# Early maxima and constants beside the second unit, one PSUM tile for the sample columns, free buffers for residual and normed rows, gates between key pieces

## The chip, the cores and the metric

The kernel runs on one core of a Trainium2 chip. The metric is the device time of one execution, in microseconds (us). Three runs of the kernel before took 2386.42, 2399.36 and 2394.37 us, median 2394.37. A further execution was taken by the hardware profiler, and all trace rows come from that one.

The engines have short names throughout: PE (TensorE, matrix products) with PEld (its weight loads, beside the products), DVE (VectorE), ACT (ScalarE), POOL (GpSimd), SP (SyncE, which here issues nearly all DMAs). Each works through its own queue in order.

## The reference

One inference step of two residual layers over a prompt of 2048 rows and a sample of 32 rows (8 sequences of 4), 1024 columns wide, in float32:

```python
def run_trunk(x, fox_attend, ...):
    for l in range(DEPTH):                   # DEPTH = 2
        if l % 2 == 0:
            out, ... = even_mixer(rmsnorm(x, norm_even[i]), w_in_even[i], ...)
        else:
            out, ... = odd_mixer(rmsnorm(x, norm_odd[i]), w_in_odd[i], ...)
        x = x + out
    return rmsnorm(x, final_norm), ...

def even_mixer(h, w_in, ...):
    qa, fa, ia, ga, qb, kb, vb, gb, fb = split(h @ w_in)
    f = lb + (1.0 - lb) * sigmoid(fa)
    o_a = head_rmsnorm(gated_linear_chunked(qa, 1 - f, ia, log(f), hgrn_s0)) * silu(ga)
    o_b = fox_attend(qb, kb, vb, log_sigmoid(fb + b_fox)) * silu(gb)
    return concatenate([o_a, o_b]) @ w_out

def odd_mixer(h, w_in, w_gate, b_gate, gla_gain, w_out, gla_s0):
    q, k, v, g, r = split(h @ w_in)
    log_f = log_sigmoid(r @ w_gate + b_gate) / 16
    o = gated_linear_chunked(q * dk ** -0.5, k, v, log_f, gla_s0)
    return (head_rmsnorm(o, gla_gain) * silu(g)) @ w_out
```

The even layer's second half is an attention with forgetting (causal softmax for the prompt, paged cache for the sample). Keys, values, log forget values and states are outputs too.

## The kernel before

**Arithmetic.** TensorE multiplies float16. An activation or weight is scaled by a power of two and written as a sum of two float16 parts, high and low; a product is three matmuls (`mm3`, L583 to L585: high by high, high by low, low by high). Splitting off the parts (one ACT copy, one DVE subtraction) is `split_evac` (L578, L579) for the first norm's rows, L1762 to L1766 for the mixer's output rows (`y_pieces`, loaded at L1752), and L348 to L356 for weights.

**Halves and units.** The prompt goes through the dense work in two halves of 1024 rows; half 0 has the 32 sample rows beside it, as columns 1024 to 1055 of the activation tile `act`. Dense work comes in *units* of some 256 output columns. A unit is a pair: four preparing steps and a run. The steps are: step 0 fetches the weights (L330), step 1 measures their maximum (four DVE reductions L295 over parts, one L297 over their results), step 2 spreads the maximum over the partitions with a matmul against the identity (`spr_...`, L282) and turns it into a power of two, and step 3 splits the weights. The run is a generator of pieces on PE: `proj_fm` (names pf_) gives features by rows, piece by piece of columns (`segs`: three of 352 in half 0, two of 512 in half 1, 24 matmuls each); `proj_tm` (names pt_) gives rows by features, 128 rows a tile in pairs of tiles, with `few_rows` for the 32 sample rows (names pS_; it first copies the sample's columns of `act` into a tile `sam`, L622, and its matmuls are L627).

In the even layer the units are taken in the order Av, Ag, Aqf, Aqf1, Bq, ... (unit 0 to unit 4 of half 0). In phase_odd, units 0 to 3 are the even layer's output projection for half 0 and units 4 to 7 that for half 1 (`out_units`: pt_o0 to pt_o3); then come the odd layer's Cv, Cqk, Cg for each of four heads, from unit 8.

**What sets the order.** The Python code is traced into a program, and a planner then orders each engine's instructions when the kernel is built: it takes them in traced order as their priority, works with planned times, and fills planned idle room with later instructions that are free to run. An instruction that nothing binds can therefore stand far ahead of its place in the code. `tc.issue_after(x)` binds what is traced inside it behind x, but only instructions of x's own engine: `last_x` (the last load of an input row) binds SP, `last_a` binds ACT, `last_v` (the last DVE subtraction of a split or copy to `sam`) binds DVE. `staged` (L1201) runs units j = a to b and deals out, between the pieces of unit j, the preparing steps of the units after it, from lists `todo` of pairs (unit, step); in unit 0 of half 0 (the case with `beside`) the list is written out by hand. `mux` interleaves two generators by shares, `drain` runs one to its end.

**Buffers.** Tiles are taken by tag from pools with a fixed number of buffers for each; a tile waits for the oldest one of its tag to be given back. In phase_odd: "c2" has 4 buffers (residual tiles `xo`, sums of the sample rows, and, under the tag "th", the results of the square sums), "c4" has 6 (first used by the odd units' queries, keys and gates), "v8" 2 (values of the odd units), "yr" 2 (loads of 1024x256 output columns, then the rows `x1r`). PSUM: "pj" 3 (the pieces of all dense units), "gr" 2, "st" 1, "o" 2.

**The places of the change.**

- *First norm* (`norm_groups`, L410): rows are loaded, squared and summed, scaled by their reciprocal root, transposed by PE in 128x128 blocks (L443) into PSUM tiles of the tags "gr" and "o" by turns, and split into the two parts with the norm's gain. The sample group has eight transposes of 32x128, each with its own pair of split_evac operations of 128x32.
- *Start of the even layer* (`phase_even`): unit 0's run goes beside the norm of half 0 (`handover`); during it, `staged` also deals out the measures of unit 1 to 3 and unit 2's spread and split. After it come the constants of the later phases (`more_consts`, L163 to L244: small loads, some 10 DVE operations on them, masks on POOL), bound behind last_x, last_a and last_v, and then units 1 and 2.
- *Normed rows* (`norm_store`, L510): units 4 to 7 are muxed with `prep(0)`, which takes half 0's rows after the first residual, nine tiles with the sample's first: load x1r (SP, L521), square sum (ACT, L527), mean and root (L406 on DVE, a power on POOL), gain (POOL, L529), split (ACT L534, DVE L535), store to a scratch (SP, L536). One step of the generator loads tile x, norms tile x-1 and splits tile x-2. Afterwards the rows come back transposed (`norm_fetch`, DMA transposes L553) as `act` for the odd units. In half 1 the same runs as `prep(1)` beside the odd units.
- *Residuals* (`out_units`, `ev`): for each pair of tiles a load of the residual (SP, L1802), an addition to the product out of PSUM (DVE, L1803, 128x512), and a store (SP, L1805).
- *Gates* (`mk_qk`): a Cqk unit runs the query pieces (evacuated by ACT, L1907), then for every segment a gate (one matmul `z`, L1893, out of "pj", with Abs on ACT, L1895, and a min on DVE, L1896), then Exp, Ln, Exp over the whole row, and then the key pieces (ACT, L1911).

Of the kernel before, what the change touches and what calls it, by code (L numbers as in the profile page):

```python
# [19 lines left out]
P = 128  # L20
D = 1024
KT = D // P
# [87 lines left out]
def drain(g):  # L110
    for _ in g:
        pass
# [11 lines left out]
class Kern:  # L124
# [286 lines left out]
    def norm_groups(self, pool, pps, act, hf, get_tile, gain, tags=("gr", "o")):  # L411
# [6 lines left out]
        def mk(grp):  # L418
# [15 lines left out]
            def turn(at=None, then=None):  # L434
                c0 = grp[0][0]
                if grp[-1][0] == HALF:
                    self.sam = None
                with ExitStack() as st:
                    for k in range(KT):
# [69 lines left out]

    def norm_store(self, pool, hf, tiles, gain):  # L510

# [25 lines left out]

        for x in range(len(todo) + 2):
            if x > 1:
                split(x - 2)  # L540
            if x < len(todo):
                load(x)
            if 0 < x <= len(todo):
                norm(x - 1)
            yield 1000
# [89 lines left out]
    def silu2(self, wp, dst, ps, n, nm, c):  # L635

        nc = self.nc
        th = wp.tile([P, 512], F32, tag="th", name=f"th_{nm}")
        nc.scalar.activation(dst, ps, AF.Copy, scale=c)
        nc.scalar.activation(th[:, :n], dst, AF.Tanh, scale=0.5)  # L640
        nc.vector.scalar_tensor_tensor(dst, th[:, :n], 1.0, dst, ALU.add, ALU.mult)
# [421 lines left out]
    def phase_even(self):  # L1063
# [4 lines left out]
        with pool("act", side="right") as ap, pool("w", side="right") as w0, pool("wl", side="right") as wp1, \  # L1068
# [31 lines left out]
            for hf in range(2):  # L1100
# [11 lines left out]
                if hf == 0:  # L1112
# [21 lines left out]
                    first = self.handover(list(zip(steps, turns)), dense(0, 1), last)  # L1134
                    drain(first)
                    with tc.issue_after(self.last_x.ins), tc.issue_after(self.last_a.ins), \
                            tc.issue_after(self.last_v.ins):
                        self.more_consts(wp)
                else:
                    self.sx_odd = self.gain_scale(self.g_odd, pps, "pj", "o")  # L1140
# [8 lines left out]
                cost = 20800.0  # L1149
                drain(dense(1, 3))  # L1150
                drain(mux(lin(0), LIN_E[hf], dense(3, 5), 2 * cost))
# [49 lines left out]
    def staged(self, us, a, b, beside=None):  # L1201
# [13 lines left out]
        for j in range(a, b):  # L1215
            if j:
                todo = [[(j + 3, 0), (j + 2, 1)], [(j + 2, 2)], [(j + 2, 3)]]
            elif beside is None:
                todo = [[(2, 0), (1, 3)], [(3, 0)], [(2, 3)]]
            else:  # L1220
                todo = [[(1, 0)], [(1, 1)], [(2, 0), (1, 2), (1, 3)], [(3, 0)], [(2, 1), (2, 2), (2, 3)]]
            for n, c in enumerate(us[j][1](self.ready.pop(j))):
# [564 lines left out]
    def out_units(self, hf, layer, act, wpool, wp, pps, x2=None, done=None):  # L1787
# [4 lines left out]
        def mk(u):  # L1792
# [3 lines left out]
            def ev(ps, g, cnt, m):  # L1796
                c0 = self.ttiles(hf)[g][0]
                c = undo[-1 if m < P else 0][:m]
                if x2 is None:
                    t = wp.tile([P, 2, 256], F32, tag="c2", name=f"xo{layer}{hf}{u}{g}")  # L1800
                    src = self.rows(hf, c0, m * cnt, layer == 0)[:, cs].rearrange("(g p) d -> p g d", g=cnt)
# [22 lines left out]
    def odd_half(self, hf, act, wpool, wp, pps, S):  # L1824
# [59 lines left out]
        def mk_qk(h):  # L1884
            def run(W):
                nm = f"C{hf}{h}"

                def gate():
                    f[h], u = c4("f" + nm), c4("u" + nm)
                    ff = f[h]  # L1890
                    for c0, m in self.segs(hf):
                        ps = pps.tile([P, 512], F32, tag="pj", name=f"z{nm}{c0}")
# [12 lines left out]
                if hf == 0:  # L1905
                    nc.vector.tensor_scalar(self.q_undo[h], c, SCALE, None, ALU.mult)
                yield from self.proj_fm(pps, act, W, 0, P, hf, lambda ps, c0, m: nc.scalar.activation(  # L1907
                    q[h][:, c0 : c0 + m], ps, AF.Copy, scale=self.q_undo[h]), nm + "q")
                gate()
                yield Z_C  # L1910
                yield from self.proj_fm(pps, act, W, P, P, hf, lambda ps, c0, m: nc.scalar.activation(  # L1911
                    k[h][:, c0 : c0 + m], ps, AF.Copy, scale=c), nm + "k")

# [26 lines left out]
    def phase_odd(self):  # L1940
# [4 lines left out]
        with pool("act2", side="right") as ap, pool("w2", side="right") as w0, pool("yr2", side="right") as y0, \  # L1945
# [104 lines left out]
            def prep(hf):  # L2050

                def tiles(c0):
                    t = wpool.tile([P, KT, 256], F32, tag="yr", name=f"x1r{hf}{c0}").rearrange("p k t -> p (k t)")
                    return t[:, :D], t[:, D:].bitcast(F16).rearrange("p (x d) -> p x d", x=2)

                return self.norm_store(wp, hf, tiles, grow)

# [103 lines left out]
```

## Time and profile before

| what | value |
|---|---|
| median of 3 runs | 2394.37 us (2386.42 to 2399.36) |
| the profiled execution | 2385.88 us |
| its span in the trace | 2384.2 us |
| mean granted TensorE clock | 0.985 |
| instructions | 58245 |
| HBM read, written | 248.73 MB, 79.63 MB |

How to read the rows that follow. The page gives busy time of each engine and the share of the span. A group reads: line, engine, operation, output<-inputs (names without their numbers), shape, xcount | busy time, mean ns of one | idle time of the engine just before them, and what ended most of it. A timeline row reads: start time in the span, busy time, engine, line, operation, output<-inputs, shape, xcount, and in brackets the idle time of the engine ahead of it with its releaser. SPq rows are DMA issues on SP's queue. A table by stretch gives, for each stretch A:B, its length and then by engine (PE, PEld, DVE, ACT, POOL) the busy time and the number of instructions, followed by the granted PE clock (1.00 is full), the mean busy share of the DMA engines as the view prints it, and GB/s.

### The profile page before, as it was taken

What the parts mean: (1) busy time and instruction counts of PE and PEld (TensorE: products, weight loads), DVE (VectorE), ACT (ScalarE), POOL (GpSimd) and SP (SyncE); (2) the same over time, 40 slices, a digit from 0 to 9 for tenths busy, and PEclk for the clock granted to TensorE, in tenths of its full rate; (3) what the DMA queues carried; (4) which work ended last, traced back from release to release, by engine and by line L of the source; (5) the groups of instructions that cost most, each with busy time, mean ns of one, the idle gap of its engine ahead of it and who ended that gap; (6) DMA issues with size and microseconds to landing.
All of it is one profiled execution on the core that took longest, in us unless ns stands there. A gap on an engine that the chain in (4) does not pass through costs nothing. (4 is left out here: it accounts for less than half of the span.)

```text
span 2384.2 us, 58245 instructions
## 1 busy us (share of the span) xinstructions
PE 2273.3 (95%) x23124; PEld 1617.0 (68%) x23124; DVE 1397.2 (59%) x3231; ACT 1092.9 (46%) x2379; POOL 815.8 (34%) x858
## 2 busy tenths in 40 slices
PE   6999999999999999999999998999899999999998
PEld 5667667864655876655446887777677676666887
DVE  7566566536654638566767444266675655557554
ACT  5334343333333226556667443446545535545333
POOL 1233324112212325234456344043552422322223
PEclk9999999999999999999999999999999999999999
DMA  6221334764441266776874767623233431115453
GB/s 199 63 86 60 93 111 138 193 167 139 144 130 55 78 203 232 241 254 204 267 237 134 248 201 226 158 77 120 83 112 97 114 104 60 43 59 160 154 191 150
DMA packets 358003, 344.89 MB, mean 145 GB/s; under 512 B 90993, under 2 KB 300722, under 8 KB 357730
## 3 DMA queue, kind: packets, MB, share of 16 engines
q1 hardware_dynamic: 356226, 336.64, 46.2%
q8 instruction: 182, 2.98, 0.5%
q0 software_dynamic: 1504, 4.52, 0.5%
q14 instruction: 91, 0.75, 0.1%
HBM read 248.73 MB, written 79.63 MB: 138 GB/s over the span
## 5 line engine op out<-in xcount | busy, mean ns | idle before, releaser
L583 PE MATMUL pt_o<-w_o,act 128*128 128x256 f16 x1024 | 282.9, 276 | 11.6 <-DVE xo L1803 9.2
L585 PE MATMUL pt_o<-w_o,act 128*128 128x256 f16 x1024 | 283.0, 276 | 4.8 <-DVE act L1766 4.1
L584 PE MATMUL pt_o<-w_o,act 128*128 128x256 f16 x1024 | 282.9, 276 | 0.0
L583 PEld LDWEIGHTS <-act 128*128 128x128 f16 x2304 | 227.7, 99 | 40.2 <-DVE xo L1803 3.8
L584 PEld LDWEIGHTS <-act 128*128 128x128 f16 x2304 | 227.7, 99 | 38.1 <-issue 7.6
L585 PEld LDWEIGHTS <-act 128*128 128x128 f16 x2304 | 227.9, 99 | 37.3 <-DVE act L1766 5.0
L749 POOL TENSOR_TENSOR kA<-kA,fA 128x512 f32<-128x512 f32 (+1 forms) x56 | 78.9, 1409 | 191.3 <-PE gl_A L715 142.7
L583 PE MATMUL pt_Cv<-w_Cv,act 128*128 128x256 f16 (+1 forms) x512 | 141.4, 276 | 0.0
L584 PE MATMUL pt_Cv<-w_Cv,act 128*128 128x256 f16 (+1 forms) x512 | 141.4, 276 | 0.0
L585 PE MATMUL pt_Cv<-w_Cv,act 128*128 128x256 f16 (+1 forms) x512 | 141.2, 276 | 0.0
L749 POOL TENSOR_TENSOR kC<-kC,fC 128x512 f32<-128x512 f32 (+1 forms) x56 | 83.5, 1492 | 151.8 <-PE gl_C L715 100.4
L1374 ACT ACTIVATE L<-L,nm,kc 128x512 f32<-128x512 f32 (+3 forms) x160 | 118.2, 741 | 37.5 <-DVE nm L1372 33.4
L1382 POOL TENSOR_SCALAR L<-L,nm 128x512 f32<-128x512 f32 (+3 forms) x160 | 98.8, 631 | 63.0 <-DVE nm L1378 22.1
L1409 ACT ACTIVATE th<-pt 128x512 f16<-128x512 f32 (+3 forms) x159 | 80.4, 527 | 61.3 <-PE pt L1402 60.3
L1410 DVE TENSOR_TENSOR tl<-pt,th 128x512 f16<-128x512 f32 (+3 forms) x159 | 94.5, 609 | 21.4 <-ACT th L1409 20.4
L1402 PE MATMUL pt<-ident,L 128*128 128x128 f32 x544 | 91.3, 280 | 6.5 <-POOL L L1382 3.8
L1402 PEld LDWEIGHTS pt<-ident,L 128*128 128x128 f32 x544 | 67.0, 144 | 32.8 <-DVE tl L1410 8.9
L1526 PEld LDWEIGHTS pkt<-ident,pgcache_fox_k 128*128 128x128 f32 x512 | 57.5, 141 | 42.6 <-issue 25.1
L1526 PE MATMUL pkt<-ident,pgcache_fox_k 128*128 128x128 f32 x512 | 74.7, 278 | 7.4 <-DVE kts L1530 5.3
L1855 ACT ACTIVATE vC<-pt_Cv,kc 128x512 f32<-128x512 f32 (+1 forms) x40 | 23.9, 599 | 123.2 <-PE pt_Cv L585 123.2
L583 PE MATMUL pt_Av<-w_Ai,act 128*128 128x256 f16 x256 | 71.1, 278 | 0.5 <-ACT act L578 0.5
L584 PE MATMUL pt_Av<-w_Ai,act 128*128 128x256 f16 x256 | 70.9, 277 | 0.4 <-DVE w_Ai L349 0.4
(952 smaller groups left out, 6752.9 us busy)
## 6 DMA issues: line engine op xcount, KB each, us to landing
pgcache_fox_k<-in_cache_fox_k SPq DMA_DIRECT2D x128, 256.0 KB, 4.3
pgcache_fox_v<-in_cache_fox_v SPq DMA_DIRECT2D x128, 256.0 KB, 4.1
yr<-yT SPq DMA_DIRECT2D x16, 1024.0 KB, 6.9
x1d<-xo SPq DMA_DIRECT2D x48, 256.0 KB, 3.6
wr_Aqf<-in_w_in_even SPq DMA_DIRECT2D x64, 128.0 KB, 3.3
wr_o<-in_w_out_even SPq DMA_DIRECT2D x32, 256.0 KB, 6.1
xo<-in_x_prompt SPq DMA_DIRECT2D x32, 256.0 KB, 3.4
wr_Cv<-in_w_in_odd SPq DMA_DIRECT2D x32, 256.0 KB, 3.8
```

The source lines that it names most:

```text
L583: nc.tensor.matmul(ps, lh[0], rh[0], start=first, stop=False)
L584: nc.tensor.matmul(ps, lh[0], rh[1], start=False, stop=False)
L585: return nc.tensor.matmul(ps, lh[1], rh[0], start=False, stop=last)
L749: nc.gpsimd.tensor_tensor(kv[:, :, 0], kv[:, :, 0], t1.to_broadcast([P, nb, w]), ALU.mult)
L1374: self.last_exp = nc.scalar.activation(lt[:, :w], lt[:, :w], AF.Exp, bias=nm[:, 0:1], scale=ib, accum_out=nm[:, 2 + j : 3 + j])
L1382: nc.gpsimd.tensor_scalar(lt[:, :w], lt[:, :w], nm[:, 1:2], 2.0**14, ALU.mult, ALU.mult)
L1402: nc.tensor.transpose(pt[:, w : w + P], rows[b][s // 4][0][:, (s % 4) * P : (s % 4 + 1) * P], self.ident)
L1409: nc.scalar.activation(th[:, a:w], pt[:, a:w], AF.Copy),
L1410: nc.vector.tensor_tensor(tl[:, a:w], pt[:, a:w], th[:, a:w], ALU.subtract)))
L1526: nc.tensor.transpose(pk[:, j * P : (j + 1) * P], pgs[j][:, h * P : (h + 1) * P], self.ident)
L1855: r = nc.scalar.activation(v[h][:, g : g + cnt], ps[:, :, :256], AF.Copy, scale=c)
```

## The change

1. `norm_groups`, sample group: eight transposes into one PSUM tile (tag "gr"), one DVE multiplication by the gain into a tile of tag "th", one ACT copy to the high part, one DVE subtraction to the low part.
2. `norm_store` gets a parameter `lead`: 1 is the order of before; half 0 takes 2, that is, each x1r row is loaded one step earlier. In half 0 the odd tiles of x1r come from the tag "v8" (two buffers) and the even ones from "yr" (two).
3. `silu2` keeps its Tanh as `last_th`.
4. `staged`: unit 0's list of half 0 loses the last three steps of unit 2; unit 1's list becomes: unit 2's measure, spread and split after its first three pieces, then the rest.
5. `phase_even`: two pieces of unit 1 are run ahead of `more_consts`; these constants are bound behind last_x, last_a and last_th (the Tanh, on ACT) instead of last_v. Unit 2 follows as before.
6. `out_units`: layer 0's residual tiles come from "c4" (six buffers) instead of "c2".
7. `mk_qk`: the gate becomes a generator; for head 0 it stops ahead of every segment but the first, so that a gate and a key piece take turns. For the other heads it runs through at once.

```diff
@@ norm_groups, turn
                 if grp[-1][0] == HALF:
                     self.sam = None
+                if c0 == HALF:
+                    n, xn = grp[0][1], xs[0]
+                    ps = pps.tile([P, 512], F32, tag=tags[0], name=f"nt{c0}")[:, : KT * n].rearrange(
+                        "p (k t) -> p k t", k=KT)
+                    for k in range(KT):
+                        nc.tensor.transpose(ps[:, k], xn[:n, k * P : (k + 1) * P], self.ident[:n, :n])
+                    t = pool.tile([P, KT, n], F32, tag="th", name=f"ng{c0}")
+                    nc.vector.tensor_tensor(t, ps, gain.unsqueeze(2).to_broadcast([P, KT, n]), ALU.mult)
+                    hi, lo = (x[:, :, c0 : c0 + n] for x in act)
+                    self.last_a = nc.scalar.activation(hi, t, AF.Copy)
+                    self.last_v = nc.vector.tensor_tensor(lo, t, hi, ALU.subtract)
+                    return
@@ norm_store
-        for x in range(len(todo) + 2):
-            if x > 1:
-                split(x - 2)
-            if x < len(todo):
-                load(x)
-            if 0 < x <= len(todo):
-                norm(x - 1)
+        for x in range(-lead, len(todo) + 1):
+            if x > 0:
+                split(x - 1)
+            if x + lead < len(todo):
+                load(x + lead)
+            if 0 <= x < len(todo):
+                norm(x)
             yield 1000
@@ silu2
-        nc.scalar.activation(th[:, :n], dst, AF.Tanh, scale=0.5)
+        self.last_th = nc.scalar.activation(th[:, :n], dst, AF.Tanh, scale=0.5)
@@ phase_even, half 0
                     drain(first)
+                    second = dense(1, 2)
+                    for _ in range(2):
+                        next(second)
                     with tc.issue_after(self.last_x.ins), tc.issue_after(self.last_a.ins), \
-                            tc.issue_after(self.last_v.ins):
+                            tc.issue_after(self.last_th.ins):
                         self.more_consts(wp)
+                    drain(second)
...
-                drain(dense(1, 3))
+                drain(dense(2 - hf, 3))
@@ staged
-                todo = [[(1, 0)], [(1, 1)], [(2, 0), (1, 2), (1, 3)], [(3, 0)], [(2, 1), (2, 2), (2, 3)]]
+                todo = [[(1, 0)], [(1, 1)], [(2, 0), (1, 2), (1, 3)], [(3, 0)]]
+            if beside and j == 1:
+                todo = [[(2, 1)], [(2, 2)], [(2, 3)], [(4, 0), (3, 1)], [(3, 2)], [(3, 3)]]
@@ out_units, ev
-                    t = wp.tile([P, 2, 256], F32, tag="c2", name=f"xo{layer}{hf}{u}{g}")
+                    if layer:
+                        t = wp.tile([P, 2, 256], F32, tag="c2", name=f"xo{layer}{hf}{u}{g}")
+                    else:
+                        t = wp.tile([P, HALF + TS], F32, tag="c4", name=f"xo{layer}{hf}{u}{g}")[:, :512].rearrange(
+                            "p (g d) -> p g d", g=2)
@@ mk_qk, gate
-                    for c0, m in self.segs(hf):
+                    for x, (c0, m) in enumerate(self.segs(hf)):
+                        if x and h == 0:
+                            yield
@@ mk_qk, run
-                gate()
+                gates = gate()
+                next(gates, None)
                 yield Z_C
-                yield from self.proj_fm(pps, act, W, P, P, hf, lambda ps, c0, m: nc.scalar.activation(
-                    k[h][:, c0 : c0 + m], ps, AF.Copy, scale=c), nm + "k")
+                for x in self.proj_fm(pps, act, W, P, P, hf, lambda ps, c0, m: nc.scalar.activation(
+                        k[h][:, c0 : c0 + m], ps, AF.Copy, scale=c), nm + "k"):
+                    next(gates, None)
+                    yield x
@@ prep
-                    t = wpool.tile([P, KT, 256], F32, tag="yr", name=f"x1r{hf}{c0}").rearrange("p k t -> p (k t)")
+                    p, tag = (wp, "v8") if hf == 0 and c0 // P % 2 else (wpool, "yr")
+                    t = p.tile([P, KT, 256], F32, tag=tag, name=f"x1r{hf}{c0}").rearrange("p k t -> p (k t)")
...
-                return self.norm_store(wp, hf, tiles, grow)
+                return self.norm_store(wp, hf, tiles, grow, 1 + (hf == 0))
```

2 lines of the change are left out of this document (1 added, 1 removed).

## Prediction

> **What bounds the kernel now.** I read the page first: the engine totals, then the groups by cost with the idle time ahead of them.
>
> ```profile
> span 2384.2 us, 58245 instructions
> PE 2273.3 (95%) x23124; PEld 1617.0 (68%) x23124; DVE 1397.2 (59%) x3231; ACT 1092.9 (46%) x2379; POOL 815.8 (34%) x858
> L583 PE MATMUL pt_o<-w_o,act 128*128 128x256 f16 x1024 | 282.9, 276 | 11.6 <-DVE xo L1803 9.2
> ```
>
> TensorE is busy 95% of the span and works from end to end, so time is won only where PE stands still or runs at a lower granted clock, and what another engine saves off that path is worth nothing. The span less 2273.3 leaves about 111 us of PE idle time in all. So I went through PE's timeline for idle stretches beside the edited lines. The third row shows one: 9.2 us of waiting for the residual add at L1803.
>
> **Unit 1's start (early maxima, constants, sample columns).**
>
> ```profile
> 44.04 0.24 PE L443 MATMUL nt<-ident,nx 32*128 32x32 f32 x1
> ...
> 44.21 0.28 PE L585 MATMUL pt_Av<-w_Ai,act 128*128 128x256 f16 x1
> ...
> 49.44 0.30 PE L443 MATMUL nt<-ident,nx 32*128 32x32 f32 x2
> 51.22 0.40 PE L627 MATMUL pS_Av<-w_Ai,sam_Av 128*32 128x256 f16 x8 [1.47 <-DVE sam_Av L622]
> 51.83 0.62 PE L627 MATMUL pS_Av<-w_Ai,sam_Av 128*32 128x256 f16 x16 [0.21 <-DVE sam_Av L622]
> 59.69 0.80 PE L282 MATMUL spr_Aqf<-ident,rm_Aqf 128*128 128x128 f32 x2 [7.24 <-DVE kc L264]
> 60.28 0.50 PE L583 MATMUL pf_Ag<-act,w_Ag 128*128 128x352 f16 x1
> ```
>
> The matmul that spreads unit 2's maximum (spr_Aqf, L282) stands in PE's queue ahead of unit 1's first product (pf_Ag) and holds it for 7.24 us. VectorE says why:
>
> ```profile
> 51.28 2.45 DVE L295 TENSOR_REDUCE rm_Aqf<-wr_Aqf 128x1 f32<-128x512 f32 x4
> ...
> 56.63 2.39 DVE L295 TENSOR_REDUCE rm_Aqf<-wr_Aqf 128x1 f32<-128x512 f32 x4
> ...
> 59.50 0.14 DVE L297 TENSOR_REDUCE rm_Aqf<-rm_Aqf 128x1 f32<-128x4 f32 x1
> ```
>
> Unit 2's four reductions are over at 53.73; the last one, which the matmul needs (L297), comes 5.8 us later, behind constants and unit 3's reductions. The change puts two column pieces of unit 1 ahead of that matmul and the constants behind them, so pf_Ag follows pS_Av directly. Saved: 7.24 us, and about 0.3 of the 0.59 that the spread takes at low clock (it stays, later). What is late next? w_Ag:
>
> ```profile
> 48.61 2.26 POOL L356 TENSOR_TENSOR w_Ag<-wr_Ag,w_Ag 128x512 f16<-128x512 f32 x2 [13.81 <-ACT w_Ag L355]
> ```
>
> It is complete at 50.87, before pS_Av's 52.45. Then the clock, from the table by stretch (length, PE busy with its matmuls, PEld, DVE, ACT, POOL, granted clock):
>
> ```profile
> 60.28:64.00 3.72, 3.72 (x18) 2.08 (x17) 3.63 (x9) 0.00 (x0) 1.38 (x5) 0.64 0.00 0
> 64.00:69.00 5.00, 5.00 (x36) 3.40 (x35) 3.94 (x21) 4.43 (x9) 3.34 (x13) 1.00 0.23 61
> ```
>
> After the wait the granted clock is 0.64: 18 matmuls took 3.72 us that at 5.00/36 = 0.139 us need 2.5. Another 1.2 us. Maxima and constants: 7.2 + 0.3 + 1.2 = 8.7 us.
>
> Sample columns: eight pairs of small evacuations, taking turns with the transposes through two PSUM buffers from 44.04 to 49.74, become three wide operations behind eight transposes in a row. Such a 128x256 operation has no row here; the nearest, L1803 with 128x512 out of PSUM, takes 0.75 us (its row stands below), so the three take at most 2.25, and the copies to sam_Av follow. If the transposes stay spread until 49.74, PE waits up to 1.6 us longer than now; put in a row at 44.04 they leave over 3 us to spare, and the waits for sam_Av (1.47 and 0.21) go. One buffer is all that a row of eight needs, so I take the latter. A transpose between matmuls holds PE for 0.17 us, two in a row took 0.30: eight together save 0 to 1.3 us, of which I take 0.7. Sum 1.7 + 0.7 = 2.4 us, the bounds -1.6 and 3.0. PE then reaches pf_Ag at 52.45 - 2.4 = 50.05; of the two instructions in w_Ag's row the first is done by then, and the second, done at 50.87, serves the later half of the first piece.
>
> A loss: the constants on VectorE are no longer held behind the sample copy, since the new bound (a Tanh) binds ScalarE alone. Unbound lines run as soon as the plan has room, as these rows show:
>
> ```profile
> 0.94 0.32 POOL L219 MEMSET bmask<- 128x256 f32 x1
> ...
> 27.75 0.16 DVE L264 TENSOR_REDUCE kc<-g_odd 128x1 f32<-128x8 f32 x1 [0.51 <-DMA g_odd<-in_norm_odd]
> ```
>
> L219 belongs to the constants and runs at 0.94. The second, hoisted from the second half, kept VectorE waiting 0.51 us for its DMA amid the first norms. Four or five more such constants (g_hgrn, g_gla, the lb maxima) can land there: 0 to 3 us; I take 1. ScalarE has three constants behind the Tanh, and nothing on PE waits for those; the DMAs stay behind the last x row on SP, the masks were unbound on GpSimd before. Unit 4's fetch moves three pieces later, with two units ahead of its use. Unit 1's start: 8.7 + 2.4 - 1.0 = **10.1 us**.
>
> **Residual and normed rows (units 4 to 7).**
>
> ```profile
> 1444.24 0.28 PE L583 MATMUL pt_o<-w_o,act 128*128 128x256 f16 x1 [3.54 <-DVE xo L1803]
> 1464.63 0.27 PE L583 MATMUL pt_o<-w_o,act 128*128 128x256 f16 x1 [2.83 <-DVE xo L1803]
> 1485.02 0.27 PE L583 MATMUL pt_o<-w_o,act 128*128 128x256 f16 x1 [2.85 <-DVE xo L1803]
> ```
> ```profile
> 1443.32 0.15 DVE L406 TENSOR_SCALAR rst_n<-nss 128x1 f32<-128x1 f32 x1 [3.58 <-ACT nsq L527]
> 1443.43 0.75 DVE L1803 SCALAR_TENSOR_TENSOR xo<-pt_o,kc,xo 128x512 f32<-128x512 f32 x1
> ```
> ```profile
> 1442.14 1.06 ACT L527 ACTIVATE nsq<-x1r 128x1024 bf16<-128x1024 f32 x1 [3.72 <-DMA x1r<-x1d]
> ```
> ```profile
> 1443.31 1.08 SPq L1802 DMA_DIRECT2D xo<-in_x_prompt  x2
> ```
>
> The rows are one chain. The residual add stands behind the norm's L406, that behind the square sum on ACT, that behind a late row load x1r; and on SP the next two residual loads go out at 1443.31, when the square sum has given back its c2 buffer. Both halves of the edit bite: residuals get six c4 buffers that nobody else uses until the odd projections, and x1r gets four buffers in place of two and is loaded one step earlier. A step of the norms is 1000 units of 11500 against 84000, 7.3 us of products, double the 3.54 us by which the worst add was late. On SP one row load moves ahead of a residual load per step (its SP row is a plain issue, and its data come from rows stored by unit 3). The borrowed v8 buffers are wanted next by the values of units 8 and 11, after their last rows are stored. Saved: 9.2 us, and the clock again:
>
> ```profile
> 1377.00:1397.00 20.00, 20.00 (x186) 17.92 (x184) 8.84 (x13) 11.02 (x20) 8.80 (x6) 1.00 0.84 257
> 1444.24:1448.24 4.00, 4.00 (x24) 3.08 (x25) 0.47 (x1) 1.15 (x1) 2.32 (x2) 0.64 0.91 299
> 1464.63:1468.63 4.00, 4.00 (x25) 3.06 (x25) 1.28 (x1) 1.16 (x2) 0.87 (x1) 0.65 0.82 238
> 1485.02:1489.02 4.00, 4.00 (x25) 3.09 (x25) 3.73 (x4) 0.23 (x1) 1.86 (x2) 0.66 1.20 232
> ```
>
> Undisturbed, 20.00/186 = 0.1075 us a matmul, 37 in 4 us. The three stretches did 24, 25 and 25: 37 missing, 4.0 us. In all 13.2; I take 12, as one wait may partly stay. Each of the three idle stretches is followed by a low clock, the two of under 3 us too.
>
> [...]
>
> A cost: six buffers let two more 256 KB residual loads go out ahead of the y rows at the start of unit 0.
>
> ```profile
> 1310.02 1.22 SPq L1802 DMA_DIRECT2D xo<-in_x_prompt  x2
> 1311.56 2.86 SPq L1752 DMA_DIRECT2D yr<-yT  x2
> ```
>
> Two issues took 1.22 us there, right before the y rows. 0 to 2 us; I take 1. Net **11 us**.
>
> **Gates between key pieces.**
>
> ```profile
> 1532.32 0.60 PE L1893 MATMUL zC<-rT,wg 80*128 80x352 f32 x2
> 1535.52 0.43 PE L1893 MATMUL zC<-rT,wg 80*128 80x352 f32 x1 [2.60 <-ACT qC L1907]
> 1536.59 0.31 PE L583 MATMUL pf_C00k<-act,w_Cqk 128*128 128x352 f16 x1 [0.63 <-DVE uC L1896]
> ```
> ```profile
> 1534.94 0.54 ACT L1907 ACTIVATE qC<-pf_C00q,kc 128x352 f32<-128x352 f32 x1
> ```
> ```profile
> 1890.63 0.38 PE L583 MATMUL pf_C10k<-act,w_Cqk 128*128 128x512 f16 x1 [1.88 <-ACT qC L1907]
> ```
> ```profile
> 1537.40:1541.40 4.00, 4.00 (x18) 2.07 (x17) 1.17 (x2) 2.89 (x3) 0.00 (x0) 0.57 0.00 0
> 1541.40:1545.40 4.00, 4.00 (x29) 2.64 (x27) 0.21 (x1) 2.92 (x3) 0.00 (x0) 1.00 0.00 0
> ```
>
> Three PSUM buffers serve queries, gates and keys in turn, so the third gate waits for the third query's evacuation (ends 1535.48). With a key piece (24 matmuls, 24 x 4.00/29 = 3.3 us) behind the first gate, the second gate asks for that buffer at about 1536.2: the wait of 2.60 is covered, the 0.63 too, and the clock's 11 missing matmuls (1.5 us). In half 1 the first key takes the first query's buffer, free long before: 1.88. Sum 6.6; I take **6.4 us**. The Exp and Ln behind the last gate start two key pieces later and lie beside the whole g unit. Above, nothing is gained if the planner sets all gates ahead of the keys again (0), and no bound lies below that: the same instructions run.
>
> **Sum.** 10.1 + 11 + 6.4 = 27.5 us. The profiled execution took 2385.88 us, span 2384.2: that becomes 2358.4. The runs' median, 2394.37, lies 8.5 higher with a spread of 13; 27.5 off it gives **2367**. About 0.5% (12 us) is what a measurement of this kernel can tell from no change.
>
> **Rivals.**
> (a) *VectorE's order keeps the adds late*: L1803 still stands behind the norms, so earlier loads free little. For it: in the first wait the stall sits on L406, not on the load. Against it: what L406 waits for is x1r. Without those 12 us: 15.5 saved, 2379. Chance 0.16.
> (b) *Constants block VectorE in the first 36 us*: one that is planned ahead of its DMA stops the norms, or spr_Aqf is planned ahead of pf_Ag after all. It gives back about the 8.7: 18.8 saved, 2376. Chance 0.10.
> (c) *The transposes come late*: with three rows in flight the last row is stored one step, 7.3 us, later.
>
> ```profile
> 1485.42 4.07 SPq L553 DMA_TRANSPOSE act<-xs  x1
> ...
> 1508.97 3.07 SPq L553 DMA_TRANSPOSE act<-xs  x1
> ```
>
> These are the first and last of half 0's eight; SP needs 26.6 us for them. If all wait for the last store, unit 8 starts 7.3 us late, and 1.3 of clock: 18.9 saved, 2375. Against it: the early tiles don't need the last row. Chance 0.07.
> (d) *Slower: SP's queue stops at residual loads.* A load planned ahead waits at SP's head until the store six pairs back has landed, and weights, rows and stores wait behind it, at each of the 32 pairs of units 0 to 7. From 27.5/32, about 0.9 us a pair, the gain is gone; at 1.5 us it costs 48, with 16.5 left of the rest: 2426. Against it: six pairs are some 30 us. Chance 0.05.
>
> **How the numbers follow.** The forecast has 0.62 (its own range 2354 to 2378). The range takes in (b), (c) and most of (a) with the spread of the runs, and the full terms on the low side: 2352 to 2386. Faster by over 0.5% (below 2382.4): 0.84; within: 0.11; slower: 0.05.
>
> **What would show it.** Right: pf_Ag starts near 50 to 51 us, no PE wait of over 1 us between 50 and 65; the waits for xo in units 4 to 7 sum to under 2 us and the clock there is 1.0; no wait over 1 us at zC or at k's first piece. Wrong: a DMA named ahead of L168 or L175 with idle PE (b); idle time ahead of pt_Cv from act<-xs (c); long SP waits at L1802 (d). New waits elsewhere of over 10 us, from the plan being made anew, would break the sum without touching its terms.

## The result and the profile after

The changed kernel takes 2364.99 us, median of four runs (2363.55 to 2367.49), against 2392.05 for the kernel before, median of its four (2386.42 to 2399.36). The ratio is 0.9887, 95% interval [0.9865, 0.9909]: 27 us faster, between 22 and 32. That is within 2 us of the forecast 2367, but the way there was not as forecast in every step. The profiled execution of the changed kernel took 2365.9 us, 20.0 less than that of before; the sum of the prediction had said 27.5 less, 2358.4. The page after:

```profile
span 2364.2 us, 58202 instructions
PE 2265.2 (96%) x23124; PEld 1613.1 (68%) x23124; DVE 1404.4 (59%) x3225; ACT 1090.3 (46%) x2372; POOL 818.6 (35%) x858
L595 PE MATMUL pt_o<-w_o,act 128*128 128x256 f16 x1024 | 281.1, 274 | 8.2 <-DVE xo L1825 6.6
```

Span less PE's busy time is 99 us of idle time (111 before), and PE's busy time is 8.1 us shorter for the same 23124 matmuls: part of the gain is clock (mean granted 0.989, 0.985 before). The row of the residual add (L1825, L1803 before) still shows 6.6 us of the 9.2. The lines have moved: L583 to L585 are L595 to L597 now, L527 is L539, L529 is L541, L535 is L547, L536 is L548.

Where the 20.0 us are is read from when the same matmul starts in the two traces:

| first matmul of | before | after | ahead by | gained in the stretch | forecast |
|---|---|---|---|---|---|
| unit 2 (pf_A00f) | 83.29 | 79.36 | 3.9 | 3.9 | 10.1 |
| pS_Bk, end of half 0's linear attention | 399.04 | 392.18 | 6.9 | 2.9 | 0 |
| phase_odd's unit 0 (pt_o) | 1305.91 | 1299.29 | 6.6 | -0.2 | 0 |
| its unit 2 | 1354.70 | 1344.91 | 9.8 | 3.2 | -1 |
| unit 8 (pt_Cv) | 1497.17 | 1481.52 | 15.6 | 5.9 | 12 |
| first key piece of half 0 (pf_C00k) | 1536.59 | 1516.95 | 19.6 | 4.0 | 4.5 |
| half 1's first query piece (pf_C10q) | 1874.94 | 1855.48 | 19.5 | -0.2 | 0 |
| half 1's second value unit | 1932.82 | 1911.35 | 21.5 | 2.0 | 1.9 |
| end of the span | 2384.2 | 2364.2 | 20.0 | -1.5 | 0 |

**Unit 1's start.** PE's rows and VectorE's in the changed kernel (columns as in the prediction):

```profile
39.45 0.69 PE L455 MATMUL nt<-ident,nx 128*128 128x128 f32 x2 [4.00 <-DVE act L591]
...
56.06 0.40 PE L639 MATMUL pS_Av<-w_Ai,sam_Av 128*32 128x256 f16 x8 [1.00 <-DVE sam_Av L634]
56.39 0.32 PE L595 MATMUL pf_Ag<-act,w_Ag 128*128 128x352 f16 x1
```
```profile
22.27 0.20 DVE L213 CAST mlev<-mtmp 128x64 int8<-128x64 f32 x1 [0.86 <-POOL mtmp L210]
...
28.37 0.17 DVE L168 TENSOR_SCALAR g_hgrn<-g_hgrn 128x4 f32<-128x4 f32 x1 [1.13 <-DMA g_hgrn<-in_hgrn_gain]
...
35.10 0.16 DVE L175 TENSOR_TENSOR lb<-lb 128x4 f32<-128x4 f32 x1 [2.99 <-DMA lb<-in_lb_logits]
```

pf_Ag now starts 0.33 us behind the first sample matmuls, as forecast; it was 9.06 behind them before. The other 16 sample matmuls now come after pf_Ag's first two products, so the fair measure is from pS_Av to unit 2: 23.3 us, 32.07 before, 8.8 less. But pS_Av itself starts 4.84 us later than before (56.06 against 51.22): VectorE runs the constants amid the first norms, waits 2.99 us for a constant's DMA at 35.10, and PE waits 4.00 at 39.45 for an evacuation.

**Units 0 to 7.** The add's waits are smaller but more, in five places:

```profile
1394.86 0.27 PE L595 MATMUL pt_o<-w_o,act 128*128 128x256 f16 x1 [0.86 <-DVE xo L1825]
1416.83 0.27 PE L595 MATMUL pt_o<-w_o,act 128*128 128x256 f16 x1 [0.85 <-DVE xo L1825]
1424.07 0.27 PE L595 MATMUL pt_o<-w_o,act 128*128 128x256 f16 x1 [1.84 <-DVE xo L1825]
1431.44 0.27 PE L595 MATMUL pt_o<-w_o,act 128*128 128x256 f16 x1 [1.96 <-DVE xo L1825]
1439.59 0.28 PE L595 MATMUL pt_o<-w_o,act 128*128 128x256 f16 x1 [1.09 <-DVE xo L1825]
```

Two chains lead to them. Timeline of the other engines ahead of 1416.83, and ahead of 1424.07:

```profile
1408.65 2.35 POOL L541 TENSOR_TENSOR x1r<-x1r,grow 128x1024 f32<-128x1024 f32 x1
...
1409.88 6.23 DVE L547 SCALAR_TENSOR_TENSOR x1r<-x1r,rsr_n 32x1024 f16<-32x1024 f32 x2 [0.35 <-ACT x1r L546]
...
1411.50 2.34 POOL L541 TENSOR_TENSOR x1r<-x1r,grow 128x1024 f32<-128x1024 f32 x1
...
1414.95 0.34 SPq L548 DMA_DIRECT2D xs<-x1r  x1
...
1416.05 0.73 DVE L1825 SCALAR_TENSOR_TENSOR xo<-pt_o,kc,xo 128x512 f32<-128x512 f32 x1
```
```profile
1416.98 0.34 SPq L533 DMA_DIRECT2D x1r<-x1d  x1
...
1420.94 1.06 ACT L539 ACTIVATE nsq<-x1r 128x1024 bf16<-128x1024 f32 x1 [3.22 <-DMA x1r<-x1d]
...
1423.16 0.15 DVE L406 TENSOR_SCALAR rst_n<-nss 128x1 f32<-128x1 f32 x1 [0.89 <-ACT nsq L539]
1423.27 0.75 DVE L1825 SCALAR_TENSOR_TENSOR xo<-pt_o,kc,xo 128x512 f32<-128x512 f32 x1
```

In the first, two splits on VectorE take 6.2 us while POOL multiplies the next rows by the gain; the add stands behind them, and so does the store L548 at SP's head. In the second, the row load behind that store lands late, ScalarE and then L406 wait for it, and the add stands behind L406, as in the kernel before. Of the 5.9 us gained, 2.6 are waits (9.2 to 6.6) and 2.4 are clock: before, all three waits were followed by a low clock (0.64 to 0.66, 37 matmuls missing), now only the one at 1431.44 is (0.57, 22 matmuls in 4 us in place of 37, so 15 missing, at 0.1075 us each). The other 0.9 I cannot place.

### The profile page after: what moved, and what is told of

Its sections match the earlier page's. It is cut to its first block, busy times and chain, and to the rows that moved or that the text cites. A ratio compares the mean times of both kernels' runs of the same rounds, so it can differ in the third digit from the quotient of the medians.

```text
span 2364.2 us, 58202 instructions
## 1 busy us (share of the span) xinstructions
PE 2265.2 (96%) x23124; PEld 1613.1 (68%) x23124; DVE 1404.4 (59%) x3225; ACT 1090.3 (46%) x2372; POOL 818.6 (35%) x858
## 5 line engine op out<-in xcount | busy, mean ns | idle before, releaser
L595 PE MATMUL pt_o<-w_o,act 128*128 128x256 f16 x1024 | 281.1, 274 | 8.2 <-DVE xo L1825 6.6
L597 PE MATMUL pt_o<-w_o,act 128*128 128x256 f16 x1024 | 281.0, 274 | 3.8 <-DVE act L1784 3.7
L597 PEld LDWEIGHTS <-act 128*128 128x128 f16 x2304 | 227.3, 99 | 39.4 <-DVE act L1784 5.1
L595 PEld LDWEIGHTS <-act 128*128 128x128 f16 x2304 | 227.4, 99 | 35.9 <-issue 3.4
L595 PE MATMUL pt_Cv<-w_Cv,act 128*128 128x256 f16 (+1 forms) x512 | 141.4, 276 | 0.0
L597 PE MATMUL pt_Cv<-w_Cv,act 128*128 128x256 f16 (+1 forms) x512 | 141.3, 276 | 0.0
L1825 DVE SCALAR_TENSOR_TENSOR xo<-pt_o,kc,xo 128x512 f32<-128x512 f32 x48 | 35.8, 748 | 62.0 <-PE pt_o L597 57.2
L597 PE MATMUL pt_Av<-w_Ai,act 128*128 128x256 f16 x256 | 70.9, 277 | 1.5 <-DVE act L591 1.5
```

The lines of the kernel that those rows point to most:

```text
L595: nc.tensor.matmul(ps, lh[0], rh[0], start=first, stop=False)
L597: return nc.tensor.matmul(ps, lh[1], rh[0], start=False, stop=last)
L1825: nc.vector.scalar_tensor_tensor(t[:m, :cnt], ps, c, t[:m, :cnt], ALU.mult, ALU.add)
```

## The experiments

"Span" is that of one profile; the ratio is to runs of the kernel before on the same chip, with its 95% interval. The last columns are the start of unit 2, and PE's waits for xo in units 4 to 7, in us.

| kernel | median us | ratio | span | unit 2 at | waits |
|---|---|---|---|---|---|
| only_early | 2386.35 | 0.9990 [0.9975, 1.0005] | 2382.8 | 81.4 | 9.7 |
| only_rows | 2374.12 | 0.9941 [0.9922, 0.9959] | 2371.9 | 83.2 | 5.9 |
| only_gates | 2382.91 | 0.9967 [0.9954, 0.9980] | 2381.6 | 83.8 | 10.1 |
| const_v | 2361.03 | 0.9876 [0.9858, 0.9893] | 2361.7 | 73.4 | 5.4 |
| only_c4 | 2385.27 | 0.9995 [0.9986, 1.0005] | 2385.3 | 83.3 | 10.3 |
| cv_no_lead | 2366.61 | 0.9916 [0.9899, 0.9933] | 2365.0 | 73.5 | 14.8 |
| cv_gain_dve | 2358.93 | 0.9888 [0.9872, 0.9905] | 2352.3 | 73.2 | 6.3 |
| cv_store_pool | 2351.95 | 0.9852 [0.9836, 0.9869] | 2354.2 | 73.2 | 4.8 |
| after_again | 2367.16 | 0.9905 [0.9885, 0.9924] | 2365.6 | 80.0 | 4.7 |
| const_again | 2357.10 | 0.9862 [0.9841, 0.9882] | 2355.0 | 73.2 | 4.0 |
| cv_rows_pool | 2359.29 | 0.9866 [0.9844, 0.9888] | 2361.9 | 73.4 | 4.7 |
| cv_both | 2358.93 | 0.9866 [0.9850, 0.9883] | 2357.0 | 73.6 | 7.5 |

The three parts alone take 0.10%, 0.59% and 0.33% off, 1.02% together; the whole change takes 1.13%. Part 1, the single tile, was not run alone.

**The constants.** My theory: the constants that the new bound sets free on VectorE delay the norms. The rival: the sample group's single tile, or the early maxima, do. *only_early* is the kernel before with parts 3, 4 and 5 of the change alone. *const_v* holds the constants on VectorE again:

```diff
                     with tc.issue_after(self.last_x.ins), tc.issue_after(self.last_a.ins), \
-                            tc.issue_after(self.last_th.ins):
+                            tc.issue_after(self.last_th.ins), tc.issue_after(self.last_v.ins):
```

> The kernel before with the early maxima and constants alone (last_th, unit 1's and 2's lists, two pieces of unit 1 ahead of the constants). Theory 1: the free constants alone delay the norms, so pS_Av starts 4 to 6 us later than before (55 to 57.5), spr_Aqf no longer waits 7.24 us, and unit 2 starts 3 to 4 us earlier than before's 83.29. Rival (the sample group's tile makes the delay): pS_Av at 51 and unit 2 at 74 to 76. Open: whether the 2.9 us that the changed kernel gains between 345 and 396 us (layer 0's linear attention) come with this part; then the span is 2377, otherwise 2380 (before 2384.2).

> The changed kernel with its constants held behind VectorE's last copy to sam too (last_v), beside last_x, last_a and last_th. Theory 1 (free constants on VectorE): in the changed kernel VectorE waits 2.99 us for lb ahead of L175 at 35.10 amid the first norms, and pS_Av starts at 56.06 instead of 51.22. With the constants held, no constant of more_consts runs on VectorE before 48 us, pS_Av starts between 48 and 51.5, unit 2's first product (pf_A00f, 79.36 in the changed kernel, 83.29 before) at 72 to 75, and the time is 5 to 7 us under the changed kernel's: 2358 to 2360. Rival (the sample group's one PSUM tile or the early maxima delay the norms, not the constants): pS_Av stays within 1 us of 56.06 and the time at 2365.

In only_early VectorE waits 3.48 us ahead of L175, at 35.77, and pS_Av starts at 58.51, 7.3 us late (4 to 6 were forecast), with the sample group still in eight pieces. The rival falls. (The 2.9 us of the linear attention came with this part, but its rows have nothing to do with it; see only_gates.) In const_v, PE and VectorE:

```profile
49.13 0.40 PE L639 MATMUL pS_Av<-w_Ai,sam_Av 128*32 128x256 f16 x8 [1.00 <-DVE sam_Av L634]
49.47 0.32 PE L595 MATMUL pf_Ag<-act,w_Ag 128*128 128x352 f16 x1
...
73.35 0.31 PE L595 MATMUL pf_A00f<-act,w_Aqf 128*128 128x352 f16 x1
```
```profile
52.48 0.15 DVE L168 TENSOR_SCALAR g_hgrn<-g_hgrn 128x4 f32<-128x4 f32 x1
...
52.62 0.15 DVE L175 TENSOR_TENSOR lb<-lb 128x4 f32<-128x4 f32 x1
```

The constants run without a wait at 52.5, and unit 2 starts 9.9 us earlier than before. The forecast was 10.1, or 11.1 without the 1 us that it set aside for the constants. Of the 9.9, 2.1 are there at pS_Av (49.13 against 51.22), from the single PSUM tile, and 7.9 come from there to unit 2. Between only_early's 58.51 and the changed kernel's 56.06 the tile brings 2.45. const_v's median was 4 us under the changed kernel's (5 to 7 were forecast), and the intervals of the ratios, 0.9876 and 0.9887, overlap: its trace gave part of the 6 us back later. So both kernels ran once more side by side:

> The changed kernel once more, beside const_again on one chip, for the price of the free constants in time: 0.989 of before's time, pS_Av at 56 us and unit 2 at 79.4 us again. What differs between its two traces where the order of the instructions is one and the same is not the change's doing: 1 to 4 us are expected, in the linear attention and at the paged cache.

> const_v once more, beside after_again. Theory 1 (the constants alone delay the norms): unit 2 at 73.4 us again, and the median 4 to 7 us under that of after_again. Rival (the 6 us are given back later, as the first trace of const_v seems to show in the attention with the cache and the linear attention): the medians within 2 us of each other.

Unit 2 starts at 80.0 and 73.2, and the medians are 10 us apart (2367.16 and 2357.10), with intervals of the ratios that just don't meet. The price of the free constants is 6 to 7 us at the place itself. In the whole time it was 2.6 us by the ratios of the first pair of runs and 10 in the second; what makes the difference is not explained.

**The parts alone.** *only_gates* has part 7 alone, *only_rows* parts 2 and 6.

> The kernel before with the gates between key pieces alone. Theory: the waits of 2.60 and 0.63 us at zC and k in half 0 and 1.88 at k in half 1 go with the low clock behind the first, 5.5 to 6.5 us in all: span 2378 (before 2384.2). Rival (the gain in half 1 is given back in the linear attention beside it, which the changed kernel shows as 22.63 us ahead at k and 21.46 a unit later): 4 to 5 us, span 2379.5.

> The kernel before with the residuals in c4 and the x1r rows a step earlier in four buffers, nothing else. The changed kernel gained 3.2 us in unit 0 and 5.9 us in units 4 to 7 there. Theory (both come from this part): the same two gains to within 1.5 us, span 2384.2 - 9 = 2375, and waits for xo (L1803 in before) that sum to 5 to 8 us in units 4 to 7. Rival (the gain in unit 0 is a by-product of the plan made anew by the earlier parts): 5.9 us only, span 2378. If the waits left in units 4 to 7 stand behind L406 and L535's split on VectorE, the adds are late by VectorE's order, as rival (a) of the prediction has it; if they stand behind loads, by SP.

At the places of the table the gates bring 4.0 us in half 0 and 2.0 in half 1, as in the changed kernel, and 0.33% in the median. Two gates now come behind the first key piece; over the whole unit, from pf_C00q to pf_C00g, half 0 gains 3.9 us in the changed kernel and 3.0 here. The span is only 2.6 us shorter, where 6 were forecast: in this trace 2.6 us of the lead are lost again between half 0's gates and half 1's, and 1.7 behind them. But the trace of only_gates is also 2.3 us ahead of before's at pS_Bk, and this kernel's instructions stand in the same order as before's until the gates at 1530 (two neighbouring small matmuls apart). Here is where that is won, in the table by stretch, before first:

```profile
371.00:376.00 5.00, 3.87 (x88) 2.89 (x89) 4.85 (x12) 0.72 (x1) 3.31 (x3) 0.75 0.30 94
376.00:381.00 5.00, 5.00 (x27) 3.46 (x26) 1.85 (x4) 0.00 (x0) 1.05 (x1) 0.56 0.18 55
```
```profile
371.00:376.00 5.00, 4.73 (x105) 3.55 (x104) 4.87 (x11) 0.72 (x1) 2.68 (x3) 1.00 0.34 111
376.00:381.00 5.00, 5.00 (x101) 4.06 (x100) 4.36 (x10) 0.69 (x1) 2.84 (x3) 1.00 0.22 65
```

Before's execution had a granted clock of 0.75 and 0.56 there, only_gates 1.00. (The counts, 27 and 101 matmuls, are not of the same work.) The same instructions, from the transpose ktS_A to where the lead stops growing, took 8.69 us in before (371.89 to 380.58) and 5.78 in only_gates (372.53 to 378.31). Net, 2.6 us are left between 360 and 399, for only_gates had its own low clock a little earlier (0.66 from 366 to 371, 1.00 in before). Every one of the other kernels gained 2.7 to 4.6 us in the stretch from unit 2 to pS_Bk. So I put the 2.9 us that the changed kernel gained there down to this one profiled execution of before, not to the change.

only_rows gained 3.7 us in units 0 and 1 and 8.1 in units 4 to 7, so both come from this part, as the theory had it, the second with 2.2 more than the changed kernel showed; its waits of 5.9 are in the forecast range. Which half of it does what, *only_c4* (part 6 alone) and *cv_no_lead* (const_v without part 2) tell:

> The kernel before with the residuals in c4 alone. Open: where the 3.2 to 3.7 us come from that the changed kernel and only_rows gain in unit 0. If from c4 (residual loads start later, so that the y rows, issued at 1311.56 behind them in before, go out ahead of them): unit 0's gain is 3 to 4 us here too. If from the earlier rows: none. Units 4 to 7: with theory 'six buffers' 5 to 8 us, with theory 'earlier rows' 0 to 3. Span 2372 to 2376 or 2379 to 2382.

> const_v without the earlier row loads and the two borrowed buffers (edit 2 undone), residuals still in c4. If the six residual buffers make the gain, units 4 to 7 gain as much as in const_v (8.8 us against before, within 1.5) and the time stays within 2 us of const_v's. If the earlier row loads make it (the waits of before end on L406, which waits for a row), the three waits of 2.8 to 3.5 us behind L406 come back, units 4 to 7 gain under 3 us, and the time is 6 to 9 us above const_v's.

The six residual buffers by themselves bring 3.0 us in units 0 and 1 and 0.5 in units 4 to 7: nothing in the median. Without the earlier rows there are five waits (14.8 us), units 4 to 7 are 3.7 us slower than before, and the ratio is 0.9916 against 0.9876 and 0.9862 of const_v's two sets of runs. So six buffers alone bring nothing in units 4 to 7; the gain there needs the rows' lead with its two borrowed buffers. The lead without c4, and the lead and the two buffers apart, were not run. The gain in unit 0 comes with c4, through SP's order. SP's queue before, then after:

```profile
1310.02 1.22 SPq L1802 DMA_DIRECT2D xo<-in_x_prompt  x2
1311.56 0.37 SPq L1752 DMA_DIRECT2D yr<-yT  x1
```
```profile
1301.05 0.37 SPq L1770 DMA_DIRECT2D yr<-yT  x1
...
1306.92 2.97 SPq L1824 DMA_DIRECT2D xo<-in_x_prompt  x4
```

The y rows now go out 1.8 us after unit 0's first product (5.7 before), ahead of the residuals, where I had expected two more residual loads ahead of them.

**What holds the adds that are left.** Theory A: VectorE's splits beside POOL's gains. Theory B: SP's queue, with row loads behind stores and residual loads. SP's waits (us in total, times, longest) in the changed kernel between 1398 and 1482 make B look strong. The second view is before's, between 1398 and 1498:

```profile
SPq L1824 <- DMA x1d<-xo: 22.2, 9, 5.9
SPq L548 <- DVE x1r L547: 9.6, 5, 4.9
```
```profile
SPq L1802 <- ACT nsq L527: 16.3, 7, 4.6
```

The six buffers changed what SP waits for at the residual loads (before, ScalarE's square sum, which held the c2 buffer; now the store of an earlier pair's sum), but not that it waits.

The three experiments start from const_v. cv_gain_dve: L541 on VectorE in half 0. cv_store_pool: L548 from POOL's queue in half 0. cv_rows_pool moves all of half 0's row work off VectorE (the split is shown; its mean, L406, goes to POOL as well). The three edits, cut to the lines that change:

```diff
-            nc.gpsimd.tensor_tensor(xt, xt, gain[:n], ALU.mult)
+            (nc.vector if hf == 0 else nc.gpsimd).tensor_tensor(xt, xt, gain[:n], ALU.mult)
```
```diff
-            nc.sync.dma_start(self.xs[dc : dc + n], t.rearrange("p x d -> p (x d)"))
+            (nc.gpsimd if hf == 0 else nc.sync).dma_start(self.xs[dc : dc + n], t.rearrange("p x d -> p (x d)"))
```
```diff
-            nc.scalar.activation(t[:, 0], xt, AF.Copy, scale=r)
-            nc.vector.scalar_tensor_tensor(t[:, 1], xt, r, t[:, 0], ALU.mult, ALU.subtract)
+            nc.scalar.activation(xt, xt, AF.Copy, scale=r)
+            nc.scalar.activation(t[:, 0], xt, AF.Copy)
+            nc.gpsimd.tensor_tensor(t[:, 1], xt, t[:, 0], ALU.subtract)
```

> const_v with half 0's gain multiplication of the normed rows on VectorE in place of POOL. In const_v the waits for xo in units 4 to 7 still sum to 5.4 us. Theory A (VectorE and POOL get in each other's way): the split L547 takes 1.28 us by itself, but 1.45 to 2.2 in const_v and up to 5.04 in the changed kernel where POOL's gain (L541, 2.35 us) runs at the same time, and POOL's pow (L408) stands behind that gain; then every L547 takes 1.3 us here, and the waits fall to under 3 us, the time 2 to 4 us under const_v's 2361. Theory B (SyncE: its queue stands at residual loads until a store has landed, so rows come late): the waits stay at 4 to 6 us and VectorE's nine more operations cost up to 2 us more.

> const_v with half 0's stores of the split rows (L548) issued by POOL's queue in place of SyncE's. Theory B (SyncE's queue is the limit: it stands 2 to 5 us at a time at the head for L548 and for residual loads, and row loads wait behind): without L548 in that queue row loads go out earlier, the waits for xo fall from 5.4 us to 2 to 4, and the time is 1 to 3 us under const_v's. Theory A (VectorE and POOL): the waits stay at 5 to 7 us, or rise, since POOL, which works on the next rows' gains, now also waits for each split; time 2360 to 2363.

> const_v with everything that half 0's normed rows do on VectorE moved off it: the mean (L406) goes to POOL, the split's scaling to ScalarE (one more 128x1024 operation a row), the subtraction to POOL. Theory (a) of the prediction (the residual adds are late because they stand behind the norms in VectorE's order, whatever makes these late: a row's load, POOL's gain or a slow split): VectorE then has no work of the rows at all, every add runs as its product ends, the waits for xo in units 4 to 7 (5.4 us in const_v, 6.6 in the changed kernel) fall under 1 us, and the time is 4 to 7 us under const_v's. Rival (the loads of the residuals themselves are late behind SyncE's waits for stores): the waits stay at 4 to 7 us. A third outcome: POOL with 5.5 us a row of 7.3 falls behind, the last rows are stored late, and PE waits for act<-xs at unit 8 instead, 2 to 6 us.

In cv_gain_dve every split takes 1.3 us, so POOL's gains are what stretches them (all instructions of the line; durations in ns, min/median/max; the changed kernel, then cv_gain_dve):

```profile
L547 DVE SCALAR_TENSOR_TENSOR x1r<-x1r,rsr_n x9: 1265/1285/5039, 1409.9 to 1452.7; 128x1024 f16<-128x1024 f32 x8, 32x1024 f16<-32x1024 f32 x1
```
```profile
L547 DVE SCALAR_TENSOR_TENSOR x1r<-x1r,rsr_n x9: 1262/1279/1286, 1402.4 to 1441.8; 128x1024 f16<-128x1024 f32 x8, 32x1024 f16<-32x1024 f32 x1
```

Yet the waits stay at 6.3 us: A is a real delay and not the bound. In cv_store_pool one wait of 4.76 us is left, and it is A's:

```profile
1425.31 3.20 DVE L547 SCALAR_TENSOR_TENSOR x1r<-x1r,rsr_n 128x1024 f16<-128x1024 f32 x1 [0.81 <-ACT x1r L546]
1428.49 3.29 DVE L547 SCALAR_TENSOR_TENSOR x1r<-x1r,rsr_n 128x1024 f16<-128x1024 f32 x1
...
1432.51 0.28 PE L595 MATMUL pt_o<-w_o,act 128*128 128x256 f16 x1 [4.76 <-DVE xo L1825]
```

cv_rows_pool should have cleared VectorE altogether, and a wait of 3.81 us remained (with one of 0.92), by another way round:

```profile
1440.29 1.06 ACT L539 ACTIVATE nsq<-x1r 128x1024 bf16<-128x1024 f32 x1 [6.75 <-DMA x1r<-x1d]
...
1442.93 0.73 ACT L348 ACTIVATE w_Cv<-wr_Cv,kc 128x544 f16<-128x544 f32 x1
```

A row lands late, ScalarE stands still for it with a weight's split behind, VectorE's half of that split (L349) starts only at 1443.77, and the add stands behind it. My rival (a), VectorE's order, is thus one form of something wider: the add stands behind work on rows or weights in an in-order queue, and some row is late. So the last kernel took both A and the store out:

> const_v with both half 0's gain on VectorE (as cv_gain_dve) and the stores of the split rows on POOL's queue (as cv_store_pool). In cv_gain_dve every split took 1.3 us, and the two waits left (3.26 and 2.17 us) ended on rows that landed late; in cv_store_pool the one wait left (4.76) stood behind two splits of 3.2 us beside POOL's gains. If these two are the whole of the rest, the waits for xo in units 4 to 7 fall under 2.5 us (4.0 and 5.5 in the two traces of const_v), units 4 to 7 gain 10 us or more against before, and the time is 2356 or less, 0.984 to 0.987 of before's. If a row's load comes late whatever the queue, as cv_rows_pool's 3.81 us at 1446 show (ScalarE and with it a weight split behind a row landed at 1440.27), 3 to 5 us of waits are left and the time is const_v's.

The forecast failed: 7.5 us of waits are left, the largest behind L406 and a row for which ScalarE waited 6.57 us; the gain in units 4 to 7 is 1.5 us. Its time is const_v's all the same. Each of A, SP's store and VectorE's order is seen to hold an add in one trace or another; taking out any one, or two, left 4.7 to 7.5 us.

What the late rows of cv_gain_dve (ahead of PE's wait at 1436.84), cv_both (1438.88) and cv_rows_pool (1446.38) have in common is a wait of their load at SP's head. SP's waits between 1425 and 1429, 1425.5 and 1430, 1431 and 1436.2:

```profile
SPq L533 <- DMA xs<-x1r: 2.7, 1, 2.7
```
```profile
SPq L533 <- DMA xs<-x1r: 2.6, 1, 2.6
```
```profile
SPq L533 <- DMA xs<-x1r: 4.2, 1, 4.2
```

The load waits until the store of an earlier split row has landed and so given back a row buffer; it goes out at 1427.98, 1429.18 and 1435.99, and ScalarE can start on the row 5.7, 6.5 and 4.3 us after that. So the four row buffers are a rival: more of them might bring these rows sooner. That was not run, and what makes the late rows late stays open.

The best of the versions are const_v's runs and cv_store_pool: const_again 0.9862 and cv_store_pool 0.9852, whose intervals overlap, against 0.9887 and 0.9905 for the changed kernel.

## Why the prediction was right, and where it wasn't

- **Early maxima: right.** 7.24 of wait, 0.3 of the spread and 1.2 of clock were forecast to go, 8.7 in all; from pS_Av to unit 2, 8.8 went in the changed kernel, 9.1 in only_early and 7.9 in const_v.
- **Sample columns: the size right, its parts not.** 2.4 forecast; 2.45 measured between only_early and the changed kernel, 2.1 between before and const_v. But the waits for sam_Av, forecast to go (1.47 and 0.21), were 1.00 and 0.40 in const_v; the rest came from PE, which was through with its transposes and products at 48.1 there (49.7 before).
- **Constants: the step that failed.** "0 to 3 us; I take 1" was bounded by the one hoisted constant of the trace, L264 with 0.51 us. The casts (L213), two gains (L168) and the lb chain followed it, several of them waiting for POOL or a DMA, 3 us at L175 alone; together they cost 7.3 us at pS_Av (only_early against before) and 6.9 (the changed kernel against const_v). It is rival (b), with its place named rightly and most of its price: I had it at 8.7 and gave it 0.10.
- **Residual and normed rows: half of the mechanism right, the size not.** 12 us were forecast and 5.9 came in the profiled execution; const_v, only_rows, after_again and const_again gained 8.1 to 8.8. "Both halves of the edit bite" is wrong for units 4 to 7: six buffers alone brought 0.5 there, and the rows' lead, with its buffers, made the gain. The forecast that the waits sum to under 2 us is wrong in all of them (4.0 to 6.6); rival (a), that VectorE's order keeps the adds late, holds for part of the rest.
- **The y rows: the wrong sign.** A loss of 1 was a gain of 3.2.
- **Rival (d): the wait is there, the price is not.** SP stands 22.2 us at residual loads, as it said (17.9 before, mostly for the square sum), but units 4 to 7 didn't get slower; the late rows that could be traced stood behind a split or a store of a row.
- **Gates: right.** 6.4 forecast, 4.0 + 2.0 measured in the changed kernel.
- **The total.** 27.5 forecast; 20.0 between the two profiled executions, of which 2.9 belong to before's clock and 1.5 were lost again near the end; 27 between the medians. The profile of before lay near the fastest of its runs (2385.88; 17 further runs spread from 2385.78 to 2396.14), that of the changed kernel among the middle of its own. In the sum, 6.2 too much for the constants and 6.1 for the rows met 4.2 of unit 0 and the 2.9 on the other side. That the median came out within 2 us of the forecast is luck, because two errors met: the profiled execution came out 7.5 above the sum, and the median lay 0.9 below that execution, where 8.5 above had been assumed.

## What to carry to other kernels

Where a planner fills idle room, moving a bound from one engine to another also frees everything on the engine that is no longer bound: list those instructions and what each waits for, and keep the old bound beside the new one. When one late load is waited for by an in-order queue, look at all that stands behind it (in cv_rows_pool ScalarE idled 6.75 us for a row, a weight's split behind it); an earlier load, with two more buffers for its rows, brought here what more buffers for the residuals did not. And take part of a profile's difference for chance: the same instructions in the same order differed by 2 to 3 us at one place between two executions.

## What the runs showed of the hardware

VectorE's split of a row (L547, f32 to f16, two inputs, 32 or 128 partitions) took 1.26 to 1.29 us in cv_gain_dve, where no multiplication of POOL (L541) runs beside it. Where it began while that multiplication was running it took 2.19 to 5.04 us in the changed kernel, and 3.20 and 3.29 in cv_store_pool. In the changed kernel the split at 1426.24 took 2.19 us and ended at 1428.43, 1.08 us after POOL's multiplication, and the one at 1436.68 did the same. The longest, 5.04 us for the sample's rows, began beside one multiplication and ended 1.08 us after the next (1409.88 to 1414.92; POOL until 1413.84). POOL's multiplication was longer as well at 1431.64, where it began during the split from 1431.31 to 1432.76: 3.32 us in place of 2.35. The residual add of 128x512, which takes one input from PSUM, kept its 0.73 to 0.75 us throughout units 0 to 7, also where it began during a multiplication of POOL (0.75 at 1408.78 and at 1423.27). What makes the split and the multiplication longer beside each other, and not the add, these traces don't show.

How long PE idles doesn't tell by itself whether the clock falls. In only_c4, 1.95 us of idling ahead of 1462.74 were followed by a granted clock of 0.57 (22 matmuls in the next 4 us), and 3.33 us ahead of 1478.37 by 1.00 (37):

```profile
1462.74:1466.74 4.00, 4.00 (x22) 2.94 (x22) 2.00 (x3) 1.91 (x3) 2.83 (x2) 0.57 0.49 135
1478.37:1482.37 4.00, 4.00 (x37) 3.58 (x37) 0.71 (x1) 1.90 (x3) 2.22 (x3) 1.00 0.35 119
```

In the changed kernel 1.84 us were followed by 1.00 and 1.96 us by 0.57:

```profile
1424.07:1428.07 4.00, 4.00 (x37) 3.57 (x37) 1.83 (x1) 3.02 (x5) 4.00 (x4) 1.00 0.94 251
1431.44:1435.44 4.00, 4.00 (x22) 2.94 (x22) 1.38 (x2) 0.15 (x2) 4.00 (x4) 0.57 0.80 208
```

No single length of idling sets these four rows apart. What else decides was not shown.
